# Another order for the first tiles of a hybrid decoder block: tokens 256 to 511 first, meta tokens later

## The chip, the cores and the metric

The kernel runs on one core of a Trainium2 chip. Its time is the device time of one execution in microseconds, and lower is better. The kernel before takes 1662.32 us (median of 3 runs, 1662.05 to 1663.47).

## What is computed

The reference is one layer of a decoder with three parallel mixers, and a SwiGLU after it. 16 meta tokens are put ahead of 1024 tokens, each of 1024 channels.

```
u = rms_norm(h, norm_mix)                       # h: 1040 x 1024
proj = u @ w_in                                 # q, k, v of two attentions, forget logits, xc, yc, gates
o_a = sliding-window attention (sinks, relative bias); o_f = forgetting attention
o_c = rg_lru(conv(xc)) * gelu(yc)               # xc, yc: 512 channels each
merged = sum over g of sigmoid(gates[g]) * (o_g @ w_branch[g])
h = h + merged @ w_out
h = h + (silu(gate) * up) @ w_ffn_out           # of rms_norm(h, norm_ffn) @ w_ffn_in
out = rms_norm(h, norm_final), meta tokens dropped
```

The change is in the first stage alone: the norm of the 1040 tokens, and the first parts of the projections to xc and yc.

## The kernel before

The tokens are cut into nine tiles: tile 0 has the 16 meta tokens, tiles 1 to 8 have 128 tokens each. For each tile `load_x` brings the rows from HBM into one of four buffers `xt` (512 KB by one DMA; tile 0 has 64 KB). `normed` takes the sum of squares on ScalarE (L297), a square root (L298) and, on VectorE, a reciprocal (L299) and two halves of x times the factor times the gain (L301, it reads `xt` and `gbc`, the gain copied to all partitions by a DMA of 512 KB). `to_feature_major` turns the tile on TensorE: four transposes of 128x128 into a PSUM bank, twice (L204); there are two such banks. Each bank is copied to `uh` on ScalarE (L118), and what is lost to the shorter type `fp32r` goes to `ul` on VectorE (L119), by a subtraction that reads PSUM and `uh`.

A product is made of three matmuls for each of eight blocks of 128 channels (`mm3`, L150): high by high, high by low, low by high. Weights are split too: `load_w` loads 128x1024 numbers (512 KB) into one of two buffers `wr`, makes the high part on ScalarE (L137) and, for the first four weight tiles, the low part on GpSimd (L138), which reads two tensors in SBUF.

`proj_chunk` makes one chunk of a projection, 24 matmuls into one of three PSUM banks, and a `sink` copies the bank out on ScalarE (L269 for x, L272 for y). FULL has the chunks of all 1040 tokens: columns 0 to 271 (tiles 0, 1, 2), 272 to 527 (tiles 3, 4) and the last 512 (tiles 5 to 8). REAL leaves the meta tokens out: 512 columns, then the last 512.

All DMAs go through one queue, issued in order by SyncE (L58). The program order of the stage before is: load tiles 0, 1, the gain, tile 2; norm and turn them; four small loads and one matmul for the bias table (L321); two weights wx; load tiles 3, 4 and norm them; x of FULL[0] with the turns of tiles 3 and 4 between; x of FULL[1]; tiles 5 and 6 and two weights wy; y of REAL[0] for the first 128 channels; tiles 7 and 8; y of REAL[0] for the second; x of FULL[2]; y of REAL[1]. Each engine runs its own list in order, but the lists are made by a scheduler that follows estimated times beside the program order: matmuls of both x weights alternate in the trace. After the stage come the recurrence beside more projections, the attentions, the merge and the feed-forward part, which are not edited.

Of the kernel before, what the change touches and what calls it, by code (L numbers as in the profile page):

```python
# [16 lines left out]
P = 128  # L17
D = 1024
KT = D // P
NM = 16  # L20
# [14 lines left out]
QA, KA, QF, KF, XC, YC, GT = 0, 4, 5, 9, 13, 17, 21  # L35
# [16 lines left out]
def hybrid_block(ctx, tc, h_in, w_in, w_v0, w_v1, w_bd, par, rows, gains, relt, onehot,  # L52
                 maskrow, cmask, w_br, w_out, w_fi, w_fo, out):
    nc = tc.nc
    act, dve, pool, pe = nc.scalar, nc.vector, nc.gpsimd, nc.tensor
# [33 lines left out]
    o_bank = lambda label="": bank("ob", 1, label)  # L89
# [6 lines left out]
    ident = cp.tile([P, P], F32, name="ident")  # L96
# [29 lines left out]
    def load_w(src, n, pl=None, tag="w", bufs=None, lo_on_pool=False):  # L126
        pl = pl or wp
        kw = {} if bufs is None else dict(bufs=bufs)
        if n == D:
            raw = wp.tile([P, n], F32, tag="wr", name=nm("wr"))  # L130
        else:
            raw = pl.tile([P, n], F32, tag=tag + "r", name=nm(tag + "r"), **kw)
        dma(raw, src)
        hi = pl.tile([P, n], F32R, tag=tag + "h", name=nm(tag + "h"), **kw)
        lo = pl.tile([P, n], F32R, tag=tag + "l", name=nm(tag + "l"), **kw)
        if lo_on_pool:
            act.activation(hi, raw, AF.Copy)  # L137
            pool.tensor_tensor(lo, raw, f32(hi), ALU.subtract)  # L138
        else:
            split(hi, lo, raw)  # L140
        return hi, lo
# [12 lines left out]
    def run(gen):  # L154
        for _ in gen:
            pass
# [41 lines left out]
    def to_feature_major(xg, n, uh, ul, off):  # L198

        for half in range(2):  # L200
            pt = tr_bank()
            for i in range(4):
                k = 4 * half + i
                pe.transpose(pt[:, i * P:i * P + n], xg[:n, k * P:(k + 1) * P], ident[:n, :n])  # L204
            src = pt.rearrange("p (i q) -> p i q", i=4)[:, :, :n]
            ks = slice(4 * half, 4 * half + 4)
            split(uh[:, ks, off:off + n], ul[:, ks, off:off + n], src)
# [9 lines left out]
    FULL = ((0, 0, 272, 0), (0, 272, 256, 272), (1, 0, 512, 528))  # L217
    REAL = ((0, NM, 512, 0), (1, 0, 512, 512))

    def proj_chunk(j, w, chunk, sink):  # L220
        c, off, n, t0 = chunk
        ps = mm_bank(f"_w{j}")
        yield from mm3(ps[:, :n], [(w[0][:, k * P:(k + 1) * P], w[1][:, k * P:(k + 1) * P],
                                    uh[c][:, k, off:off + n], ul[c][:, k, off:off + n]) for k in range(KT)])
        sink(ps, n, t0)
# [36 lines left out]
    def x_sinks(pl, m):  # L262
        xr = pl.tile([P, 3 + T], F32, tag="xr", bufs=4, name=nm("xr"))
        y = pl.tile([P, S], F32, tag="y", bufs=4, name=nm("y"))
        pool.memset(xr[:, 0:3], 0.0)
        lru_in[m] = (xr, y)

        def xsink(ps, n, t0):
            act.activation(xr[:, 3 + t0:3 + t0 + n], ps[:, :n], AF.Copy)  # L269

        def ysink(ps, n, t0):
            act.activation(y[:, t0:t0 + n], ps[:, :n], AF.Copy)  # L272
        return xsink, ysink
# [3 lines left out]
    with tc.tile_pool(name="r0", bufs=1, side="right", reuse_waits="tile") as r0:  # L277
        gbc = r0.tile([P, D], F32, name="gbc")

        def rows_of(t):  # L280
            return (NM, 0) if t == 0 else (P, NM + (t - 1) * P)

        def load_x(t):
            n, t0 = rows_of(t)
            xt = r0.tile([P, D], F32, tag="xt", bufs=4, name=nm("xt"))
            dma(xt[:n], h_in[t0:t0 + n])
            return xt

        def norm_in(t, xt):
            to_feature_major(*normed(t, xt))  # L290

        def normed(t, xt):
            n, t0 = rows_of(t)
            c, off = (0, t0) if t0 < W0 else (1, t0 - W0)
            xg = r0.tile([P, D], F32, tag="xg", bufs=3, name=nm("xg"))
            q = cp.tile([P, 1], F32, tag="sq", bufs=4, name=nm("sq"))
            act.activation(xg[:n], xt[:n], AF.Square, accum_out=q[:n])  # L297
            act.activation(q[:n], q[:n], AF.Sqrt, bias=epst[:n], scale=1.0 / D)  # L298
            dve.reciprocal(q[:n], q[:n])  # L299
            for x, y, z in zip(*(halves(v[:n]) for v in (xg, xt, gbc))):  # L300
                dve.scalar_tensor_tensor(x, y, q[:n], z, ALU.mult, ALU.mult)  # L301
            return xg, n, uh[c], ul[c], off

        xts = [load_x(t) for t in range(2)]
        dma(gbc, gains[0:1].partition_broadcast(P))
        xts.append(load_x(2))
        n0, n1 = normed(0, xts[0]), normed(1, xts[1])
        to_feature_major(*n1)
        n2 = normed(2, xts[2])
        to_feature_major(*n0)  # L310
        to_feature_major(*n2)

        dma(cmt, cmask)
        rt = r0.tile([32, 8], F32, name="rt")
        oh = r0.tile([32, 383], F32, name="oh")
        mr = r0.tile([8, 383], F32, name="mr")
        dma(rt, relt)
        dma(oh, onehot)
        dma(mr, maskrow.partition_broadcast(8))
        pb = sc_bank()  # L320
        pe.matmul(pb[:8, :383], rt, oh, start=True, stop=True)  # L321
        dve.tensor_tensor(mr, pb[:8, :383], mr, ALU.add)
        sinks = [x_sinks(ra, m) for m in range(2)]
        wx = [load_w(w_in[XC + m], D, r0, f"x{m}", lo_on_pool=True) for m in range(2)]
        xs34 = [load_x(t) for t in (3, 4)]
        n34 = [normed(t, xs34[t - 3]) for t in (3, 4)]
        for m in range(2):
            run(proj_chunk(XC + m, wx[m], FULL[0], sinks[m][0]))
            if m == 0:
                to_feature_major(*n34[0])  # L330
                to_feature_major(*n34[1])
        for m in range(2):
            run(proj_chunk(XC + m, wx[m], FULL[1], sinks[m][0]))
        xs56 = [load_x(t) for t in (5, 6)]
        wy = [load_w(w_in[YC + m], D, lo_on_pool=True) for m in range(2)]
        for t in range(5, 7):
            norm_in(t, xs56[t - 5])
        run(proj_chunk(YC, wy[0], REAL[0], sinks[0][1]))
        for t in range(7, 9):
            norm_in(t, load_x(t))  # L340
        dma(part, par)
        dma(rowt, rows.partition_broadcast(P))
        dve.tensor_scalar(nsink, rowt[:, 0:8], -1.0, None, ALU.mult)
        dma(bts, mr)
        pad(r0, 32)
        bb = r0.tile([P, 8, 383], F32, name="bb")
        dma(bb, bts.partition_broadcast(P))
        dma(bss, bb)
        run(proj_chunk(YC + 1, wy[1], REAL[0], sinks[1][1]))
        for m in range(2):  # L350
            run(proj_chunk(XC + m, wx[m], FULL[2], sinks[m][0]))
        for m in range(2):
            run(proj_chunk(YC + m, wy[m], REAL[1], sinks[m][1]))
# [868 lines left out]
```

## Time and profile before

| | |
|---|---|
| median of the runs | 1662.32 us |
| the profiled execution | 1662.29 us |
| its span (first to last instruction) | 1660.5 us |
| TensorE busy with matmuls | 1630.2 us, 98% |
| VectorE, ScalarE, GpSimd busy | 60%, 46%, 26% |
| TensorE's first instruction | 9.07 us |
| TensorE's first projection matmul | 15.39 us |
| mean granted clock of TensorE | 0.996 |

The span is shorter than the execution by 1.8 us, which lie ahead of the first and behind the last instruction. In the rows below a time is the start in microseconds from the span's start, then follow the duration, engine, line and operation, with the tile written, an arrow and the tiles read. Brackets give how long the engine was idle before and what ended that.

### The profile page before, as it was taken

The numbers are of one execution on the slowest core, as the hardware profiler recorded it, in microseconds if no ns is written. First come the engines' busy times: TensorE is split into PE (matmuls) and PEld (weight loads), VectorE is DVE, ScalarE is ACT, GpSimd is POOL, SyncE is SP. The second block draws the span as 40 slices with busy tenths as digits, with TensorE's granted clock in tenths as the row PEclk, the third lists the DMA queues.
The fourth block names the chain that finished last, engine by engine and source line by source line (L and its number), as shares of the span: only waits on it lengthen the run. The fifth ranks groups of instructions, "written<-read, shape, count | busy, mean of one in ns | idle before, by whom it ended". The sixth has DMA issues, their size and how long they took to land.

```text
span 1660.5 us, 22597 instructions
## 1 busy us (share of the span) xinstructions
PE 1630.2 (98%) x8159; PEld 1375.1 (83%) x8159; DVE 999.4 (60%) x1799; ACT 760.7 (46%) x1397; POOL 433.1 (26%) x341
## 2 busy tenths in 40 slices
PE   7999999999999999999999999899999999999998
PEld 6898978888888888888887888688888888888886
DVE  6565556555566666641348437977666676567544
ACT  6456466555555555542336434333333333345342
POOL 2111001001122221110225001776666566300000
PEclk9999999999999999999999999899999999999999
DMA  7132352223324142339737221464444443598642
GB/s 255 63 108 93 122 153 79 88 89 121 108 76 129 59 122 79 107 114 320 244 127 235 102 77 70 158 222 169 165 147 146 146 161 131 197 356 278 195 128 101
DMA packets 110879, 242.47 MB, mean 146 GB/s; under 512 B 11944, under 2 KB 23544, under 8 KB 110512
## 3 DMA queue, kind: packets, MB, share of 16 engines
q1 hardware_dynamic: 110768, 241.04, 42.7%
q8 instruction: 64, 1.05, 0.3%
q14 instruction: 47, 0.39, 0.1%
HBM read 163.45 MB, written 72.21 MB: 142 GB/s over the span
## 4 chain that ended last, share of the span: by engine, by line
PE 87%; DVE 4%; issue 4%; ACT 2%; POOL 1%; DMA 1%; SPq 0%; DVEq 0%; POOLq 0%; ACTq 0%
PE mm_w L150 26%; PE mm_s L150 13%; PE tr_s L150 7%; PE mm_br L150 6%; PE mm_wo L150 5%; PE mm_x L1086 4%; PE tr_y L1086 4%; PE sc_y L1086 4%; PE ob L547 3%; PE sc_s L150 3%; PE tr L558 3%; PE mm_v L150 2%; PE ob_x L1086 1%; PE mm_g L150 1%; PE mm_u L150 1%
## 5 line engine op out<-in xcount | busy, mean ns | idle before, releaser
L150 PE MATMUL mm_w<-uh,wh 128*128 128x512 f32 (+2 forms) x744 | 292.6, 393 | 0.0
L150 PE MATMUL mm_w<-uh,wl 128*128 128x512 f32 (+2 forms) x744 | 280.5, 377 | 0.0
L150 PE MATMUL mm_w<-ul,wh 128*128 128x512 f32 (+2 forms) x744 | 279.9, 376 | 0.0
L150 PEld LDWEIGHTS mm_w<-uh,wl 128*128 128x128 f32 x744 | 140.0, 188 | 25.7
L150 PEld LDWEIGHTS mm_w<-uh,wh 128*128 128x128 f32 x744 | 140.4, 189 | 12.7
L150 PEld LDWEIGHTS mm_w<-ul,wh 128*128 128x128 f32 x744 | 140.7, 189 | 11.7
L119 DVE TENSOR_TENSOR ab<-raw,ab 128x1024 fp32r<-128x1024 f32 x77 | 93.0, 1224 | 71.6 <-ACT ab L118 69.6
L118 ACT ACTIVATE ab<-raw 128x1024 fp32r<-128x1024 f32 x77 | 80.9, 1059 | 94.7 <-PE ob_x L1086 23.4
L150 PE MATMUL mm_s<-pt,ar 128*128 128x512 f32 x480 | 117.4, 394 | 3.7 <-ACT c L952 3.7
L118 ACT ACTIVATE wh<-wr 128x1024 fp32r<-128x1024 f32 (+1 forms) x85 | 72.7, 856 | 103.2 <-PE mm_w L150 50.6
L150 PE MATMUL mm_br<-o,wh 128*128 128x512 f32 x384 | 118.3, 389 | 0.0
L119 DVE TENSOR_TENSOR pl<-tr,ph 128x384 fp32r<-128x384 f32 (+2 forms) x160 | 87.4, 555 | 47.0 <-ACT ph L118 43.1
L150 PEld LDWEIGHTS mm_s<-pt,ar 128*128 128x128 f32 x480 | 91.5, 191 | 23.6 <-ACT c L952 4.5
L118 ACT ACTIVATE ph<-tr 128x384 fp32r<-128x384 f32 (+2 forms) x160 | 76.8, 485 | 53.6 <-PE tr L558 51.5
L119 DVE TENSOR_TENSOR wl<-wr,wh 128x1024 fp32r<-128x1024 f32 x45 | 55.6, 1235 | 72.2 <-ACT wh L118 71.9
L648 POOL TENSOR_SCALAR s<-s,sm 128x144 f32<-128x144 f32 (+3 forms) x64 | 48.6, 761 | 172.1 <-DVE sm L647 144.2
L150 PEld LDWEIGHTS mm_br<-o,wh 128*128 128x128 f32 x384 | 72.1, 188 | 14.9
L558 PE MATMUL tr<-ident,s 128*128 128x128 f32 x480 | 79.6, 274 | 1.2 <-POOL s L596 0.6
L150 PE MATMUL mm_wo<-woh,hl 128*128 128x512 f32 x256 | 79.1, 390 | 0.0
L150 PE MATMUL mm_br<-o,wl 128*128 128x512 f32 x192 | 75.3, 392 | 1.5 <-DVE wl L119 1.4
L558 PEld LDWEIGHTS tr<-ident,s 128*128 128x128 f32 x480 | 59.1, 140 | 18.3 <-DVE pl L119 3.4
L1086 PE MATMUL mm_x<-ab 128*128 128x512 f32 x297 | 72.7, 389 | 0.0
(252 smaller groups left out, 3687.9 us busy)
## 6 DMA issues: line engine op xcount, KB each, us to landing
wr<-w_in_dram SPq DMA_DIRECT2D x45, 512.0 KB, 3.7
wr<-w_fi_dram SPq DMA_DIRECT2D x44, 512.0 KB, 3.8
raw<-asp SPq DMA_DIRECT2D x77, 256.0 KB, 3.2
asp<-a SPq DMA_DIRECT2D x66, 256.0 KB, 2.5
gz<-z SPq DMA_DIRECT2D x48, 256.0 KB, 2.1
o<-osp SPq DMA_DIRECT2D x24, 512.0 KB, 6.1
sg<-gz SPq DMA_DIRECT2D x48, 256.0 KB, 3.2
fo<-w_fo_dram SPq DMA_DIRECT2D x22, 512.0 KB, 5.1
```

Source lines behind the costliest of these rows:

```text
L118: act.activation(hi, src, AF.Copy)
L119: i = dve.tensor_tensor(lo, src, f32(hi), ALU.subtract)
L150: pe.matmul(ps, a, b, start=first and i == 0, stop=i == n - 1, skip_group_check=not first)
L547: pe.matmul(ob[:, q0:q0 + b - a], vt[:, c], x[:, a:b], start=count == 0, stop=count == n_mm - 1, skip_group_check=True)
L558: pe.transpose(tb[:, col:col + P], src, ident)
L648: pool.tensor_scalar(s[:, :nk], s[:, :nk], den, 1.0, ALU.mult, ALU.mult)
L1086: pe.matmul(banks[x], a[:, 0, q], b[:, 1], start=first and j == 0 and c == 0, stop=j == NJ - 1 and c % 3 == 2, skip_group_check=True)
```

## The change

Tiles 3 and 4 are loaded, normed and turned first, and x of FULL[1] is projected before the other tiles are used. The two weights wx are loaded behind tile 4, ahead of tiles 0, 1 and 2; then come tiles 1, 2 and 0, with the two weights wy loaded ahead of them. y of tokens 256 to 511 comes next, then the small loads and the matmul of the bias table, x of FULL[0], tiles 5 to 8, and y of tokens 0 to 255: the 512-column chunk REAL[0] of y has become two of 256. Besides, TensorE gets 32 transposes into a PSUM bank that nobody reads: 16 of the identity matrix at the beginning, and 8 of the normed tile after each of tiles 3 and 4.

```diff
-        xts = [load_x(t) for t in range(2)]
+        def busy(x, n, k):
+            for i in range(k):
+                pe.transpose(spare[:, :n], x[:n, i * P:(i + 1) * P], ident[:n, :n])
+
+        spare = o_bank("_spare")
+        for _ in range(16):
+            busy(ident, P, 1)
+
+        xts = {3: load_x(3)}
         dma(gbc, gains[0:1].partition_broadcast(P))
-        xts.append(load_x(2))
-        n0, n1 = normed(0, xts[0]), normed(1, xts[1])
-        to_feature_major(*n1)
-        n2 = normed(2, xts[2])
-        to_feature_major(*n0)
-        to_feature_major(*n2)
+        xts[4] = load_x(4)
+        wx = [load_w(w_in[XC + m], D, r0, f"x{m}", lo_on_pool=True) for m in range(2)]
+        sinks = [x_sinks(ra, m) for m in range(2)]
+        for t in (3, 4):
+            n = normed(t, xts[t])
+            to_feature_major(*n)
+            busy(n[0], P, 8)
+        xts = {t: load_x(t) for t in range(3)}
+        wy = [load_w(w_in[YC + m], D, lo_on_pool=True) for m in range(2)]
+        for m in range(2):
+            run(proj_chunk(XC + m, wx[m], FULL[1], sinks[m][0]))
+        for t in range(1, 3):
+            norm_in(t, xts[t])
+        norm_in(0, xts[0])
+        for m in range(2):
+            run(proj_chunk(YC + m, wy[m], (0, 272, 256, 256), sinks[m][1]))
...
-        sinks = [x_sinks(ra, m) for m in range(2)]
-        wx = [load_w(w_in[XC + m], D, r0, f"x{m}", lo_on_pool=True) for m in range(2)]
-        xs34 = [load_x(t) for t in (3, 4)]
-        n34 = [normed(t, xs34[t - 3]) for t in (3, 4)]
         for m in range(2):
             run(proj_chunk(XC + m, wx[m], FULL[0], sinks[m][0]))
-            if m == 0:
-                to_feature_major(*n34[0])
-                to_feature_major(*n34[1])
+        for t in range(5, 9):
+            norm_in(t, load_x(t))
         for m in range(2):
-            run(proj_chunk(XC + m, wx[m], FULL[1], sinks[m][0]))
-        xs56 = [load_x(t) for t in (5, 6)]
-        wy = [load_w(w_in[YC + m], D, lo_on_pool=True) for m in range(2)]
-        for t in range(5, 7):
-            norm_in(t, xs56[t - 5])
-        run(proj_chunk(YC, wy[0], REAL[0], sinks[0][1]))
-        for t in range(7, 9):
-            norm_in(t, load_x(t))
+            run(proj_chunk(YC + m, wy[m], (0, NM, 256, 0), sinks[m][1]))
...
-        run(proj_chunk(YC + 1, wy[1], REAL[0], sinks[1][1]))
```

## Rows read from the trace of the kernel before

**Rows 1.** The page's first part, TensorE's share of the span, and the first line of the chain of work that ended last.

```profile
PE 1630.2 (98%) x8159; PEld 1375.1 (83%) x8159; DVE 999.4 (60%) x1799; ACT 760.7 (46%) x1397; POOL 433.1 (26%) x341
PE 87%; DVE 4%; issue 4%; ACT 2%; POOL 1%; DMA 1%; SPq 0%; DVEq 0%; POOLq 0%; ACTq 0%
```

**Rows 2.** The table of waits of TensorE over the whole span: who waited for whom, us in total, times, longest.

```profile
PE tr L204 <- DVE xg L301: 9.1, 1, 9.1
...
PE tr L204 <- DVE ul L119: 0.5, 1, 0.5
```

**Rows 3.** The timeline of TensorE from 9 to 16 us: all up to the first projection matmuls.

```profile
9.07 1.94 PE L204 MATMUL tr<-ident,xg 128*128 128x128 f32 x8 [9.07 <-DVE xg L301]
10.94 1.44 PE L321 MATMUL sc<-oh,rt 32*8 32x383 f32 x2
12.31 3.25 PE L204 MATMUL tr<-ident,xg 16*128 16x16 f32 x16
15.39 0.59 PE L150 MATMUL mm_w<-uh,x0h 128*128 128x272 f32 x1
15.78 0.43 PE L150 MATMUL mm_w<-uh,x1h 128*128 128x272 f32 x1
```

**Rows 4.** The timeline of VectorE from 0 to 21 us, the instructions of the first norms and turns.

```profile
6.86 2.73 DVE L301 SCALAR_TENSOR_TENSOR xg<-xt,sq,gbc 16x512 f32<-16x512 f32 x4 [0.45 <-DMA gbc<-gains_dram]
10.14 0.16 DVE L299 RECIPROCAL sq<-sq 128x1 f32<-128x1 f32 x1 [0.55 <-ACT sq L298]
10.34 0.75 DVE L301 SCALAR_TENSOR_TENSOR xg<-xt,sq,gbc 128x512 f32<-128x512 f32 x1
11.01 0.68 DVE L119 TENSOR_TENSOR ul<-tr,uh 128x512 fp32r<-128x512 f32 x1
11.61 0.74 DVE L301 SCALAR_TENSOR_TENSOR xg<-xt,sq,gbc 128x512 f32<-128x512 f32 x1
12.27 0.68 DVE L119 TENSOR_TENSOR ul<-tr,uh 128x512 fp32r<-128x512 f32 x1
...
16.22 0.69 DVE L119 TENSOR_TENSOR ul<-tr,uh 128x512 fp32r<-128x512 f32 x1 [0.16 <-ACT uh L118]
```

**Rows 5.** The timeline of ScalarE, of the same stretch: the square of tile 2, the copies out of the transposes' banks, and the high parts of the weights (those of wy are from 24 us on).

```profile
8.63 1.06 ACT L297 ACTIVATE xg<-xt 128x1024 f32<-128x1024 f32 x1 [2.42 <-DMA xt<-h_in_dram]
...
10.19 0.60 ACT L118 ACTIVATE uh<-tr 128x512 fp32r<-128x512 f32 x1
11.04 0.60 ACT L118 ACTIVATE uh<-tr 128x512 fp32r<-128x512 f32 x1 [0.26 <-PE tr L204]
11.54 1.05 ACT L137 ACTIVATE x0h<-wr 128x1024 fp32r<-128x1024 f32 x1
...
14.74 0.60 ACT L118 ACTIVATE uh<-tr 128x512 fp32r<-128x512 f32 x1
...
24.57 1.05 ACT L137 ACTIVATE wh<-wr 128x1024 fp32r<-128x1024 f32 x1
```

**Rows 6.** The timeline of SyncE's queue from 0 to 60 us: when DMAs were issued.

```profile
4.47 0.83 SPq L58 DMA_DIRECT2D wr<-w_in_dram  x2
6.73 6.00 SPq L58 DMA_DIRECT2D xt<-h_in_dram  x4
15.05 2.67 SPq L58 DMA_DIRECT2D wr<-w_in_dram  x2
```

**Rows 7.** From the view of the tile wr, in stretches that hold one issue each: the time from issue to landing of the first weight load (issued at 4.47) and of the third (issued at 15.05).

```profile
DMA to landing us min/median/max: 5.7/5.7/5.7
...
DMA to landing us min/median/max: 4.2/4.2/4.2
```

**Rows 8.** The table by stretches of 1 us: busy time of PE, PEld, DVE, ACT and POOL, granted clock, DMA share and GB/s.

```profile
8.00:9.00 1.00, 0.00 (x0) 0.00 (x0) 1.00 (x3) 0.37 (x1) 0.00 (x0) 1.00 1.03 347
9.00:10.00 1.00, 0.93 (x5) 0.96 (x6) 0.59 (x1) 0.97 (x3) 0.00 (x0) 1.00 1.02 418
```

**Rows 9.** Timelines of TensorE in short stretches: a transpose alone and three in a row early on, eight in a row later.

```profile
10.59 0.42 PE L204 MATMUL tr<-ident,xg 128*128 128x128 f32 x1
...
14.28 0.85 PE L204 MATMUL tr<-ident,xg 128*128 128x128 f32 x3
...
20.64 1.03 PE L204 MATMUL tr<-ident,xg 128*128 128x128 f32 x8
```

**Rows 10.** Timelines of TensorE in short stretches: pairs of projection matmuls, of 272 columns early and later, of 256 and of 512 columns.

```profile
16.73 0.43 PE L150 MATMUL mm_w<-uh,x0h 128*128 128x272 f32 x1
16.96 0.43 PE L150 MATMUL mm_w<-ul,x0h 128*128 128x272 f32 x1
...
19.45 0.35 PE L150 MATMUL mm_w<-uh,x0h 128*128 128x272 f32 x1
...
19.89 0.28 PE L150 MATMUL mm_w<-uh,x0h 128*128 128x272 f32 x1
20.01 0.29 PE L150 MATMUL mm_w<-ul,x0h 128*128 128x272 f32 x1
...
25.49 0.28 PE L150 MATMUL mm_w<-ul,x0h 128*128 128x256 f32 x1
25.61 0.28 PE L150 MATMUL mm_w<-uh,x0l 128*128 128x256 f32 x1
...
32.34 0.39 PE L150 MATMUL mm_w<-uh,wl 128*128 128x512 f32 x1
32.57 0.39 PE L150 MATMUL mm_w<-uh,wh 128*128 128x512 f32 x1
```

**Rows 11.** Timelines of GpSimd (the low parts of the weights) and of VectorE in the stretch of the last two.

```profile
12.67 2.35 POOL L138 TENSOR_TENSOR x0l<-wr,x0h 128x1024 fp32r<-128x1024 f32 x1 [11.28 <-ACT x0h L137]
14.99 2.37 POOL L138 TENSOR_TENSOR x1l<-wr,x1h 128x1024 fp32r<-128x1024 f32 x1
25.70 2.42 POOL L138 TENSOR_TENSOR wl<-wr,wh 128x1024 fp32r<-128x1024 f32 x1 [8.33 <-ACT wh L137]
28.07 2.86 POOL L138 TENSOR_TENSOR wl<-wr,wh 128x1024 fp32r<-128x1024 f32 x1
...
28.59 2.88 DVE L301 SCALAR_TENSOR_TENSOR xg<-xt,sq,gbc 128x512 f32<-128x512 f32 x1
```

## The prediction

> **What bounds the kernel now.** I read the page's busy shares and chain first, then TensorE's waits, then the first 35 us engine by engine. TensorE is busy 98% of the span and holds 87% of the chain [rows 1]: nearly every microsecond in which it has no useful work, or does it slowly, is on the path, and one that is won early reaches the end unless a later wait takes it back. Its longest wait of all is the first, 9.1 us for the first normed half tile; the other wait of this stage is 0.5 us [rows 2]. The front costs more than the 9.1 us. Up to the first projection matmul at 15.39 TensorE runs only 24 transposes (tiles 1, 0 and 2) and the bias-table matmul [rows 3]. [...]
>
> What sets 15.39 is a chain with tile 2 at its end, not the weights. The gain lands at 6.86, and VectorE makes the four halves of tiles 0 and 1 (2.73 us) [rows 4]. Tile 2 lands just before 8.63 [rows 5]; its halves are made at 10.34 and 11.61, each with a low part of tile 1 behind it, up to 12.95 [rows 4]. These low parts free the two transpose banks. Tile 0 passes through the banks next, and the copy of tile 2's first half ends at 15.34 (14.74 + 0.60) [rows 5], 0.05 us ahead of the matmul. The low weight part x0l was done at 15.02 (12.67 + 2.35) [rows 11], only 0.4 us earlier.
>
> **The change part by part.** All terms are against the profiled execution, 1662.29 us (span 1660.5 and 1.8 around it); it lies 0.03 us below the median of 1662.32, so no correction is made.
>
> (a) The first matmul. The new chain has two tiles and no tile 0 between them. In front of tile 4 the queue now moves tile 3 and the gain, 1024 KB; before, 64 + 512 + 512 = 1088 KB stood ahead of tile 2, at 350 to 420 GB/s [rows 8] a difference of 0.2 us, so tile 4 lands at about 8.4. Square, root and reciprocal take what they took (8.63 to 10.30), so its halves are made at about 10.1 and 11.4, alternating with tile 3's low parts as at 10.34 to 12.95 [rows 4]. Tile 3's first low part frees a bank at 11.5; four cold transposes 0.21 us apart ((0.85 - 0.42) / 2; the first and the last of three, [rows 9]) and their latency, a copy of 0.60: the first half is ready for matmuls at about 13.4. The first weight now has 1536 KB ahead of it instead of 1725, which at the same rate is 0.5 us; it landed at 10.2 (4.47 + 5.7, [rows 6, 7]), so now at 9.7; ScalarE took it only at 11.54, behind copies [rows 5]. With the same delay x0l ends at about 14.5, without it 13.2. The third matmul or so needs x0l. On TensorE the eight dummy transposes of tile 4 stand ahead of the matmuls in the program: cold 8 x 0.21 = 1.7 us. Those that fit between the turns of tile 4's halves are free, the others are not: if all run behind its second half, the first matmul is at about 15.1. Between 13.4 and 15.1 I take the middle, 14.2: -1.2 us. The other dummies cost nothing: 16 x 0.21 = 3.4 us lie before the first norm (TensorE is idle to 9.07), and tile 3's eight lie before tile 4's turns.
>
> (b) Slow matmuls. From 15.39 to 19.45 there are 16 matmuls (the first 3 with waits, 13 at 0.23) [rows 3, 10], worth 16 x 0.122 = 1.95: 2.1 us lost. [...]
>
> (c) Work that lay ahead of the first matmul and now lies behind it. Tiles 1 and 2 change places with 3 and 4: nothing. Tile 0's eight small turns and the two bias-table matmuls now run in dense time: at least 8 x 0.05 + 2 x 0.3 = 1.0, half of what they took cold (the two matmuls started 0.6 apart), at most 8 x 0.11 + 2 x 0.3 = 1.5: +1.2.
>
> (d) y in two chunks. Before, 48 matmuls of 512 columns, 0.23 apart; after, 96 of 256, 0.12 apart [rows 10]: 96 x 0.12 - 48 x 0.23 = 11.5 - 11.0, from the unrounded starts +0.6. The two more copies are ScalarE's and are hidden by the next chunk.
>
> (e) The wait of 0.5 us [rows 2] stood between tiles 5 and 6, where low weight parts held VectorE up; tiles 5 to 8 now come after GpSimd has done them: -0.5, at worst 0.
>
> (f) SyncE. wy0 and wy1 wait for the buffers that x0l and x1l free (before: issued at 15.05 and 17.4, [rows 6]); the bias-table loads and tiles 5 to 8 queue behind them. The table is read in the attentions, far behind; tiles 5 to 8 are due only after 96 matmuls of y and x and 24 transposes, 14 us of TensorE. Tile 2 waits for tile 3's buffer, free at about 8. Nothing on the path: 0, at worst the second rival.
>
> (g) VectorE beside GpSimd. A multiply of L301 takes 0.75 us, but 2.88 while GpSimd makes a low weight part, ending 0.55 after it; a low part of L119, which reads PSUM, stays at 0.69 in such a stretch [rows 4, 11]. Tiles 1 and 2 are now normed while x1l and wy's low parts are made, up to 2.1 us late each. The 48 x matmuls (6 to 10 us) cover it: 0, at worst +2.
>
> Sum: -1.2 - 0.3 + 1.2 + 0.6 - 0.5 = -0.2, so 1662.1 us: the start that is won is paid back by what was moved behind it. With (a) from -2.0 to +1.1 (an x0l that ends at 14.5 or a half of tile 4 held up by it as in (g)), (c) from 1.0 to 1.5 and (e), (g) at their bounds, this case reaches from 1660.5 to 1664.5.
>
> **The rivals.** First: the dummies raise the clock. [...] For it: TensorE would have work from about 1.6 us on. Against it: before, transposes and two small matmuls filled most of 9.07 to 15.39 without any rise, and the rise came after 4 us of projection matmuls [rows 3, 10]. [...] The trace agrees as far as it goes, but its early transposes are broken by gaps and small tiles, so I leave the rival a quarter.
>
> Second, on the slower side: TensorE waits for y's weights. y of tokens 256 to 511 stands ahead of x of FULL[0] in the program. TensorE is through with 48 x matmuls and 24 turns at about 14.2 + 4.1 + 29 x 0.12 + 2.4 = 24.2. wy0 is issued when x0l is done (13.2 to 14.5), lands 4.2 later [rows 7], needs 1.05 on ScalarE and 2.4 on GpSimd [rows 5, 11]: 20.9 to 22.2 if ScalarE takes it at once. But ScalarE also has three squares, five copies and the weights then, and before it took wy0 only at 24.57, with the low part done at 28.1 [rows 5, 11]. The point is 24.2; at 28.1 the wait is 3.9 us: 1666.0. Against it: the scheduler can put x of FULL[0] first.
>
> Third, the change doesn't do what it says: the scheduler puts the tiles or dummies in another order, for instance all dummies at cold speed into time with work, 1664; or a later stage is planned otherwise, up to 3 us either way.
>
> **How the numbers follow.** Forecast 0.54, the clock 0.24, y's weights 0.13, another order 0.09. What a measurement of this kernel can tell from no change is 0.2%, 3.3 us: below 1659.0 or above 1665.6. Faster: a third of the clock case (with a start at 13.4, or less moved behind it), 0.08, half of the other order, 0.04, and 0.06 of the forecast's own edge: 0.18. Slower: half of the wait case and a third of the other order, 0.10, and 0.04 of the forecast: 0.14. No change: 0.68. The range holds the clock case nearly whole and half of the wait case: 1658.6 to 1665.4.
>
> **What would show it.** (a): the first mm_w of 256 columns at 13.4 to 15.1. (b): its successors 0.21 apart for some 4 us, then 0.12; 0.12 from the first says that the dummies raised the clock. (c), (d): 96 y matmuls of 256 columns 0.12 apart, and tile 0's turns between dense work. (e): no TensorE wait on ul near tiles 5 and 6. (g): multiplies of over 2 us beside x1l or wl. The second rival would be an idle TensorE between 20 and 28 us, ended by GpSimd's wl. I am wrong if TensorE's first 45 us hold over 3.3 us more or less useful work than before, or if the difference arises after that.

## The result, and the profile after

The kernel after the change takes 1667.68 us, the median of 6 executions (1666.36 to 1669.16); the kernel before beside it on the same chip takes 1662.18 (6 executions, 1660.75 to 1663.47). The ratio is 1.0034, 95% interval 1.0021 to 1.0047. The forecast was 1662.1 and its range ended at 1665.4: the change costs 5.5 us where none were expected, and the prediction is wrong. The profiled executions have spans of 1665.3 and 1660.5 us, so 4.8 of the 5.5 us can be looked for in the two traces; the profiled execution of the kernel after (1667.10 us) lies 0.6 below the median of its six.

TensorE's line on the page, beside [rows 1]:

```profile
PE 1635.5 (98%) x8239; PEld 1382.5 (83%) x8239; DVE 1000.2 (60%) x1799; ACT 760.9 (46%) x1399; POOL 434.8 (26%) x341
```

It holds 80 pairs of weight load and matmul more (32 transposes that nobody reads, 48 matmuls from y in two chunks), and 5.3 us more of busy time. The table of TensorE's waits (us in total, times, longest), beside [rows 2]:

```profile
PE tr L204 <- DVE ul L119: 3.8, 2, 2.3
...
PE tr L204 <- DVE xg L301: 2.2, 1, 2.2
...
PE sc L590 <- DVE sm L592: 1.3, 1, 1.3
```

The first wait of 9.1 us has become one of 2.2, but two new waits on low parts (ul) have come, and one in an attention. Three places follow from that. The first is the wait of 2.3 us; the timeline of ScalarE from 7 to 16 us, beside [rows 5]:

```profile
8.84 0.30 ACT L298 ACTIVATE sq<-sq,epst 128x1 f32<-128x1 f32 x1
9.04 1.04 ACT L137 ACTIVATE x0h<-wr 128x1024 fp32r<-128x1024 f32 x1
10.64 1.06 ACT L137 ACTIVATE x1h<-wr 128x1024 fp32r<-128x1024 f32 x1 [0.56 <-DMA wr<-w_in_dram]
11.61 1.06 ACT L118 ACTIVATE uh<-tr 128x512 fp32r<-128x512 f32 x2
12.56 1.06 ACT L297 ACTIVATE xg<-xt 128x1024 f32<-128x1024 f32 x1
...
13.70 0.60 ACT L118 ACTIVATE uh<-tr 128x512 fp32r<-128x512 f32 x1
14.76 0.60 ACT L118 ACTIVATE uh<-tr 128x512 fp32r<-128x512 f32 x1 [0.47 <-PE tr L204]
```

In this stretch ScalarE works its list in order: tile 3's transposes were through at 9.3, but their copies (11.61) stand behind both high weight parts, and x1h waits 0.56 us for its DMA with the copies behind it. Tile 4's copies (13.70, 14.76) stand behind the square of tile 1 (12.56) too, but that cost next to nothing: the first four transposes of tile 4 ended only at 13.66. VectorE's timeline, beside [rows 4]:

```profile
9.37 1.42 DVE L301 SCALAR_TENSOR_TENSOR xg<-xt,sq,gbc 128x512 f32<-128x512 f32 x2
12.22 1.29 DVE L119 TENSOR_TENSOR ul<-tr,uh 128x512 fp32r<-128x512 f32 x2 [1.44 <-ACT uh L118]
14.33 0.69 DVE L119 TENSOR_TENSOR ul<-tr,uh 128x512 fp32r<-128x512 f32 x1 [0.82 <-ACT uh L118]
...
17.94 5.40 DVE L301 SCALAR_TENSOR_TENSOR xg<-xt,sq,gbc 128x512 f32<-128x512 f32 x2
...
24.83 1.27 DVE L119 TENSOR_TENSOR ul<-tr,uh 128x512 fp32r<-128x512 f32 x2
```

Tile 4's halves are ready at 10.8 (9.37 + 1.42), earlier than tile 2's were, but the two transpose banks come free only with the low parts that start at 12.22. And at 17.94 the two multiplies of tile 2 take 5.40 us in place of 1.42. GpSimd makes the low parts of y's weights just then:

```profile
17.60 5.19 POOL L138 TENSOR_TENSOR wl<-wr,wh 128x1024 fp32r<-128x1024 f32 x2 [2.29 <-ACT wh L137]
```

What TensorE saw of both, beside [rows 3] (the timeline of TensorE; x8 and the like are instructions in one stretch):

```profile
9.06 1.63 PE L307 MATMUL ob_spare<-ident,xg 128*128 128x128 f32 x9
12.96 0.70 PE L204 MATMUL tr<-ident,xg 128*128 128x128 f32 x4 [2.27 <-DVE ul L119]
...
15.66 0.56 PE L150 MATMUL mm_w<-uh,x0h 128*128 128x256 f32 x1
...
25.56 0.66 PE L204 MATMUL tr<-ident,xg 128*128 128x128 f32 x4 [1.55 <-DVE ul L119]
```

The first projection matmul comes at 15.66, not at 14.2; and a second stop of 1.55 us comes at 24 us, ahead of tile 2's turns. The third place lies 220 us later. SyncE's queue and VectorE in the kernel before:

```profile
235.11 0.33 SPq L58 DMA_DIRECT2D wr<-w_in_dram  x1
...
237.15 2.17 SPq L58 DMA_DIRECT2D v<-vs  x2
...
243.19 0.37 DVE L586 CUSTOM_DVE_ANT_0 s<-sc,nb,nsink 128x144 f32<-128x144 f32 x1 [1.73 <-DMA nb<-bss]
```

and in the kernel after, 2.7 us later by the clock of the trace:

```profile
237.80 0.98 SPq L58 DMA_DIRECT2D wr<-w_in_dram  x1
...
239.84 3.06 SPq L58 DMA_DIRECT2D v<-vs  x2
...
247.84 0.37 DVE L592 CUSTOM_DVE_ANT_0 s<-sc,nb,nsink 128x144 f32<-128x144 f32 x1 [3.69 <-DMA nb<-bss]
```

One issue of a weight load holds SyncE 0.98 us instead of 0.33 and the next two 3.06 instead of 2.17; so the first bias block nb, which the attention's first scores need, is issued 0.9 us later against the rest (242.95 instead of 239.37, where the weight load came 2.7 later), and VectorE can use it 4.9 us after its issue instead of 3.8. VectorE waits 2 us longer for it, and TensorE 1.3 us for VectorE (the third row of the waits above). The instructions and their order are the same in both kernels from about 50 us on, on every engine.

Two measures sum this up. The first splits TensorE's time up to the first matmul of x's last chunk (512 columns, program line 351 of before), from the start times of all its records. The second is the lag: the start of an instruction of TensorE less the start of the same one (counted from the last) in the kernel before.

```
TensorE to x's last chunk, us    start+dummies+idle  transposes  bias table     x      y    sum
before                                  9.70            9.46        1.37     14.12  11.73  46.38
after                                  14.12            8.52        0.74     12.36  13.06  48.81

lag of after, us, at    60 us: 2.78    230: 2.69    260: 4.22    560: 5.40    760: 5.22    end: 4.81
```

So 2.7 us come from the front, 1.5 from the place near 244 us, and 0.6 from small steps behind it. 2.43 of the front's 2.7 us are there when x's last chunk starts (48.81 less 46.38). Split at the first projection matmul they are: that matmul +0.27; x -1.75; y +1.33; the stop of 1.55 new and one of 0.53 gone; the rest, the turns of tile 0 and the bias table that moved behind it, +1.56.

### The profile page after: what moved, and what is told of

It is laid out like the page before. It is cut to its first block, busy times and chain, and to the rows that moved or that the text cites. A ratio compares the mean times of both kernels' runs of the same rounds, so it can differ in the third digit from the quotient of the medians.

```text
span 1665.3 us, 22764 instructions
## 1 busy us (share of the span) xinstructions
PE 1635.5 (98%) x8239; PEld 1382.5 (83%) x8239; DVE 1000.2 (60%) x1799; ACT 760.9 (46%) x1399; POOL 434.8 (26%) x341
## 3 DMA queue, kind: packets, MB, share of 16 engines
q8 instruction: 65, 1.06, 0.3%
## 5 line engine op out<-in xcount | busy, mean ns | idle before, releaser
L150 PEld LDWEIGHTS mm_s<-pt,ar 128*128 128x128 f32 x480 | 91.0, 190 | 22.6 <-ACT c L958 3.6
```

Of the source, the lines that this page charges most:

```text
L150: pe.matmul(ps, a, b, start=first and i == 0, stop=i == n - 1, skip_group_check=not first)
```

## The experiments

Ten kernels ran. The table gathers them; pairs are TensorE's instruction pairs more than before, the step is the lag at 260 us less that at 230, all from one profiled execution each, and the ratio, from all executions, is to the kernel before on the same chip. Executions of one kernel lie 2 to 5 us apart from the fastest to the slowest, so the lags of a single one are not its median: start_dummies_old_order ends 0.24 us behind in the profiled execution, the fastest of its 11, and 2.0 behind in the median.

```
                             first mm  x's last  lag at  step at  lag at   pairs   ratio, 95% interval
                                         chunk    60 us    244      end
before                         15.39     46.38     0        0        0        0
after                          15.66     48.81    2.78     1.53     4.81     80    1.0034 [1.0021, 1.0047]
dummies_in_old_order           16.24     45.03   -1.35     0.03    -0.92     32    0.9996 [0.9987, 1.0004]
no_dummies                     13.19     47.27    1.24     0.64     4.01     48    1.0016 [1.0008, 1.0025]
copies_first                   13.60     49.46    3.42     1.81     5.92     80    1.0041 [1.0027, 1.0055]
low_on_vectore                 16.09     48.23    2.19     1.44     3.15     80    1.0015 [1.0006, 1.0024]
both_waits                     13.72     46.38    0.35     1.33     0.66     80    1.0009 [1.0001, 1.0018]
y_in_two_old_order             16.43     45.83   -0.52     1.02     0.41     80    1.0006 [0.9997, 1.0015]
more_dummies                   15.81     49.93    3.90     0.49     5.31     96    1.0026 [1.0015, 1.0036]
more_dummies_low_on_vectore    15.88     48.36    2.33     0.04     3.39     96    1.0023 [1.0014, 1.0033]
both_waits_more_dummies        14.03     49.15    3.12     0.01     2.20     96    1.0014 [1.0006, 1.0023]
start_dummies_old_order        17.31     47.30    0.92     0.51     0.24     36    1.0015 [1.0006, 1.0024]
```

**The dummies alone, and the order alone.** The first pair splits the change in two. dummies_in_old_order adds to the kernel before only

```
+        spare = o_bank("_spare")
+        for _ in range(16):
+            busy(ident, P, 1)
         ...
         to_feature_major(*n1)
+        busy(n1[0], P, 8)
         ...
         to_feature_major(*n2)
+        busy(n2[0], P, 8)
```

> The kernel before with the 32 transposes that nobody reads added (16 of the identity at the beginning, 8 after the turn of tile 1, 8 after that of tile 2) and nothing moved. Theory A (the new order costs the time, by two waits: tile 3's copies queue behind the second weight's high part on ScalarE, and tile 2's multiplies are held up by GpSimd's low parts): the dummies are harmless or help a little, by raising the clock before 19.5 us: 1660 to 1663, ratio to before 0.999 to 1.0005. Rival B (the dummies cost it, by standing ahead of real work on TensorE and by longer code): 1664 to 1668. Rival C (the 2.4 us that the changed kernel loses between 220 and 700 us, where its instruction order is the old one, come from moved code positions): then this kernel too, whose TensorE list is 64 instructions longer, shows a shift that grows by 1 to 3 us there; by A it grows by under 1.

It took 1661.01 us, ratio 0.9996: no difference that can be told, by the profile 0.9 us ahead. no_dummies is the kernel after without them:

```
-        spare = o_bank("_spare")
-        for _ in range(16):
-            busy(ident, P, 1)
         ...
-            busy(n[0], P, 8)
```

> The changed kernel without the 32 transposes that nobody reads. Without them the scheduler puts tile 3's copies ahead of the second weight's high part on ScalarE. Theory A: the first projection matmul comes at 13 to 14 us instead of 15.7, but at the lower clock for about 4 us, and tile 2's turn still waits for a low part of GpSimd, so TensorE's start of x of FULL[2] comes at 47.5 to 49.5 (48.8 changed, 46.4 before): 1665 to 1668. Rival B (the dummies cost it): back to 1661 to 1663.

It took 1664.91 us, 2.5 behind before's 1662.37 in that comparison. x's last chunk came at 47.27, just ahead of what I expected. So the new order loses without the dummies too, though not all of it: 2.5 us by the medians where the kernel after lost 5.5 (4.0 and 4.8 by the profiles). In the old order the dummies cost nothing that can be told; in the new one the kernel with them is the slower. The run also showed two things of the prediction. Without the dummies the scheduler puts tile 3's copies ahead of x1h, and the first matmul comes at 13.19: dummies that TensorE has time for change the plan of the other engines. And TensorE then waits 1.29 us for GpSimd's low part of y's weights, the prediction's second rival, at a third of its price:

```profile
23.20 0.38 PE L150 MATMUL mm_w<-uh,wl 128*128 128x256 f32 x1 [1.29 <-POOL wl L138]
```

**ScalarE's list.** copies_first moves two things in ScalarE's list, x1h behind tile 3's copies and the squares of tiles 1 and 2 behind tile 4's:

```
+                with tc.issue_after(last):
+                    act.activation(x1h, raw1, AF.Copy)
         ...
-            norm_in(t, xts[t])
+            with tc.issue_after(last):
+                n = normed(t, xts[t])
+            to_feature_major(*n)
```

> The changed kernel with ScalarE's order pinned: the second weight's high part x1h behind tile 3's copies, the squares of tiles 1 and 2 behind tile 4's copies. Theory A: the first projection matmul comes at 13.0 to 14.0 instead of 15.66 and the clock, once up at 10 us, stays up; but tile 2's turn still waits for GpSimd's last low part, so most is lost again there: start of x of FULL[2] at 47.5 to 49 (48.8 changed), time 1665.5 to 1668. If ScalarE's order were the whole cause, x of FULL[2] would start at 46 or earlier and the time would be 1662 to 1664.5.

The first matmul came 2.1 us earlier (13.60), yet the kernel stayed as slow, 1668.21 us. Its VectorE and GpSimd timelines say where it went:

```profile
17.79 5.36 DVE L303 SCALAR_TENSOR_TENSOR xg<-xt,sq,gbc 128x512 f32<-128x512 f32 x2
```

```profile
17.45 5.15 POOL L140 TENSOR_TENSOR wl<-wr,wh 128x1024 fp32r<-128x1024 f32 x2 [2.21 <-ACT wh L139]
```

Now tile 1 is the one held up, and TensorE, earlier by 2 us, waits 1.06 us for its first half and 2.13 us for its second:

```profile
20.55 0.63 PE L206 MATMUL tr<-ident,xg 128*128 128x128 f32 x4 [1.06 <-DVE xg L303]
...
23.30 1.09 PE L206 MATMUL tr<-ident,xg 128*128 128x128 f32 x4 [2.13 <-DVE sq L301]
```

ScalarE's list is not the whole cause. The clock did not come as expected either: up at 12.72 us, not 10, and down again from 22.96 to 26.38, beside the second of these stops.

**VectorE held by GpSimd.** low_on_vectore makes y's low parts on VectorE:

```
-        wy = [load_w(w_in[YC + m], D, lo_on_pool=True) for m in range(2)]
+        wy = [load_w(w_in[YC + m], D) for m in range(2)]
```

> The changed kernel with the low parts of the two weights wy made on VectorE instead of GpSimd. Theory A: no multiply of tile 2 of over 2 us any more, TensorE's wait of 1.55 us before tile 2's turn goes, start of x of FULL[2] at 46.8 to 47.6 (48.8 changed): 1665 to 1666.5, 1 to 2 us below the changed kernel. If the wait has another cause (ScalarE's copies, late loads), it stays and the time with it: 1667 to 1668.

The stop of 1.55 us went, and the kernel took 1664.57 us: some 3 us better than after by the ratios, still 2.2 behind before. The first stop (2.27 us at 10.70) stayed. But x's last chunk came at 48.23, not at 46.8 to 47.6. Much of what the stop gave back went to the clock: in this execution it rose at 5.38 us, fell at 8.79 and was back only at 19.03, 2.9 us after the first matmul (16.09), so that x took 13.15 us instead of 12.36. Two rows of the table by stretches (busy shares and counts of PE, PEld, DVE, ACT, POOL; granted clock, DMA share, GB/s):

```profile
9.00:10.00 1.00, 1.00 (x5) 0.63 (x3) 0.81 (x2) 1.00 (x2) 0.00 (x0) 0.50 1.10 352
...
18.00:19.00 1.00, 1.00 (x6) 1.00 (x6) 1.00 (x2) 1.00 (x3) 0.00 (x0) 0.50 1.04 150
```

The 11 executions of this kernel have mean granted clocks from 0.994 (this one) to 0.998, so the time at the lower clock differs between executions of one kernel. both_waits puts the last two edits together.

> Two edits of the kernel after together: the two of copies_first, and y's first weights split on VectorE as in low_on_vectore. Theory (two waits in series, ScalarE's list before the first projection matmul and VectorE held by GpSimd before tile 2's turn, and each hides what the other's removal brings): first projection matmul at 13.6 as in copies_first, the waits of 1.06 and 2.13 us at 19.5 and 21.2 us gone, so the first matmul of x's last chunk at 49.46 - 3.2 = 46.3 us or earlier (a drop of the clock at 23 us would go too, up to 1.5 us more), level with before's 46.38. Rival (the wait only moves on to another producer): that matmul stays later than 48 us. The step of 1.5 us near 244 us stays in either case, since the 80 more instruction pairs stay: end 1.4 to 2 us behind before.

x's last chunk starts at 46.38, before's own figure. One stop of 1.21 us is left, at 21.2 us, for tile 2's multiplies, which now stand behind a weight's low part in VectorE's own list. At x's last chunk the edit of ScalarE's list alone lost 0.65 us against after (49.46 against 48.81), the one of VectorE alone won 0.58, and both together won 2.43. The multiplies in both_waits, run beside no GpSimd:

```profile
21.52 1.41 DVE L303 SCALAR_TENSOR_TENSOR xg<-xt,sq,gbc 128x512 f32<-128x512 f32 x2
```

The two waits stand in series on the same path. Without the first alone, the second grew (from 1.55 to 3.19 us in two stops); without the second alone, TensorE still stopped at 10.7 us, and the low clock took half of the gain (0.79 of 1.55 us). Together the clock rose at 12.80, ahead of the first matmul, and stayed up. The lag at the end, 0.66, is less than I expected (1.4 to 2), since 0.5 us are won back between 540 and 600 us and as much between 1040 and 1080; the median was 1663.67, 0.95 us behind before's 1662.72.

**The step at 244 us.** With the front even, both_waits has it still, dummies_in_old_order has not. A packet of 16 KB on a queue of instructions (q8 on the page; the times of single packets are read from the trace) falls within about 1 us ahead of the slow weight-load issue: in after it starts at 236.80 and takes 1.37 us. In before the nearest are at 229.20 and 253.04. The page counts 64 such packets before and 65 after:

```profile
q8 instruction: 64, 1.05, 0.3%
```

```profile
q8 instruction: 65, 1.06, 0.3%
```

That is one per 255 instructions of TensorE (2 x 8159 / 64), and 253 in after (2 x 8239 / 65), so the packets are taken for fetches of TensorE's code; that is an inference from these counts, no run shows it alone. If it holds, more pairs at the front make a later fetch fall earlier in the work: the eleventh packet of the span starts 17.9 us behind the issue in before (253.04 and 235.11) and 1.0 ahead of it in after (236.80 and 237.80). y_in_two_old_order tests it: the old order, the old loads, the same 80 pairs.

```
-        run(proj_chunk(YC, wy[0], REAL[0], sinks[0][1]))
+        run(proj_chunk(YC, wy[0], (0, 272, 256, 256), sinks[0][1]))
+        run(proj_chunk(YC, wy[0], (0, NM, 256, 0), sinks[0][1]))
```

(the same for wy[1], and the 32 dummies of dummies_in_old_order).

> The kernel before with 32 transposes that nobody reads (as in dummies_in_old_order) and y's first 512 columns in two chunks: 80 more pairs of instructions on TensorE than before, as many as after has, with the old order of tiles and loads. Theory (the step near 244 us comes from where the fetches of TensorE's code fall): the lag on before is about -1.35 + 1.3 = 0 at 60 us, rises by 1.5 us between 230 and 260 us, and ends near +1.5. Rival (the step comes from the new order of the loads): no step, lag from 0 at 60 us to between 0 and +0.5 at the end. Apart from that the run measures y in two chunks: 0.6 us by the prediction, 1.3 by the account of after.

The step came, 1.02 us against 0.03 with 32 pairs, with the same marks on SyncE and VectorE. It is smaller than the 1.5 that I expected, and so is the lag at the end, 0.41; the kernel took 1662.88 us beside before's 1662.72:

```profile
234.53 1.20 SPq L58 DMA_DIRECT2D wr<-w_in_dram  x1
```

```profile
244.07 0.37 DVE L599 CUSTOM_DVE_ANT_0 s<-sc,nb,nsink 128x144 f32<-128x144 f32 x1 [3.19 <-DMA nb<-bss]
```

It also prices y in two chunks: y's matmuls take 12.20 us instead of 11.75, and x's last chunk comes 0.8 us later. more_dummies goes the other way, 16 pairs more than after, with 24 dummies behind tile 3:

```
-            busy(n[0], P, 8)
+            for _ in range(3 if t == 3 else 1):
+                busy(n[0], P, 8)
```

> The kernel after with 24 instead of 8 transposes that nobody reads behind tile 3. Theory (the wait of 2.28 us at 10.7 us is ScalarE's and VectorE's and stays, but TensorE filled over it keeps the full clock): first projection matmul 15.5 to 16.2, no fall of the clock at 13.45, first matmul of x's last chunk 1 to 2 us earlier than after's 48.81. With 96 more pairs than before the code fetch comes some 4 us earlier by the theory of the code's place: the step between 230 and 260 us falls from 1.5 to under 0.7. Rival (the step comes with any lag of TensorE): it stays 1.5. Rival on the clock (transposes don't hold it): it falls near 13 us as in after and the last chunk is as late, or later by the 16 transposes' time.

> As more_dummies, and y's first weights split on VectorE as in low_on_vectore. Theory: both the wait before tile 2's turn (1.55 us) and the slow clock go: first matmul of x's last chunk at 46 to 47 us, the level of before (46.38), and no step near 244 us, so an end within 1 us of before's. Rival (what is won in one place is waited for in the next): that matmul stays at 48 us or later, the end 2 us or more behind before's.

The second has low_on_vectore's edit too. The steps are 0.49 and 0.04 us with lags of 3.84 and 2.29 at 230 us, so a late TensorE alone does not make the step. The issue in the second is quick again, and the wait short:

```profile
237.39 0.33 SPq L58 DMA_DIRECT2D wr<-w_in_dram  x1
```

```profile
245.68 0.37 DVE L593 CUSTOM_DVE_ANT_0 s<-sc,nb,nsink 128x144 f32<-128x144 f32 x1 [1.93 <-DMA nb<-bss]
```

Over all kernels: with 80 pairs that issue takes 0.58 to 1.20 us and the step is 1.0 to 1.8, in either order; with any other count it takes 0.33 and the step is 0 to 0.64; that load lands 4.9 to 6.5 us after its issue with 80 pairs and 3.8 to 4.1 with others. With 96 pairs the packet falls near as well, but it has ended 0.7 us or more ahead of the issue; with 80 it is still running then, or has just ended (both_waits, 0.13 us ahead, with the shortest of the slow issues, 0.58). What makes the small ones (0.49 to 0.64) is open: there the issue is quick, but nb lands late all the same. The fronts of these two kernels missed: x's last chunk came 1.1 us later than in after in the one, 0.45 earlier in the other, whose rival came true (48.36, and 3.4 us behind before at the end). The scheduler answered the longer list with other places for ScalarE's work: in more_dummies the square of tile 2 too went ahead of tile 4's copies, and TensorE waited 0.52 us for its first matmul and 1.01 us two matmuls later, with the clock down again from 18.28 to 21.69.

**Two tries at a kernel better than both.** both_waits_more_dummies is both_waits with 26 dummies at the start and 14 behind tile 4; start_dummies_old_order is the kernel before with 36 at the start and no others.

```
-        for _ in range(16):
+        for _ in range(26):
             busy(ident, P, 1)
         ...
             busy(n[0], P, 8)
+            if t == 4:
+                busy(n[0], P, 6)
```

> As both_waits, with 26 instead of 16 transposes that nobody reads ahead of tile 3 (over the 2.3 us in which TensorE waited at 5.1 us) and 14 instead of 8 behind tile 4 (over the wait for the first projection matmul): 96 more instruction pairs than before, as in more_dummies_low_on_vectore. Theory of the code's place: the step between 230 and 260 us, 1.33 us in both_waits, falls under 0.3. First matmul of x's last chunk at 45.5 to 46.4 us (the clock rises earlier, the producers set the rest), so an end 0.3 to 1.2 us ahead of before's. Rival (the step belongs to the new order with a front as fast as before's): it stays near 1.3, the end 0.5 to 1 us behind before's. Rival on the front: six more transposes ahead of the first projection matmul push it by 0.6 us and all behind it.

```
+        for _ in range(36):
+            busy(ident, P, 1)
```

> The kernel before with 36 transposes of the identity that nobody reads at the very start and none behind the tiles: the old order alone, with TensorE busy from 1.4 to 9 us. Theory (the transposes pay by the clock alone, and the old order is as good as the new): the clock rises ahead of 12.8 us, the first projection matmul comes ahead of dummies_in_old_order's 16.24, by 15.4 as before's or earlier, and the first matmul of x's last chunk 0.3 to 1 us ahead of dummies_in_old_order's 45.03; 36 more pairs, no step near 244 us; end 1 to 2 us ahead of before's. Rival (VectorE and ScalarE set the old front and not TensorE): the last chunk stays at 45 us or later, the end within 1 us of before's.

Neither is faster than before. In the first the step is gone (0.01 us), as foretold, which a rival tied to the new order does not allow; but VectorE's list had a weight's low part (1.23 us) ahead of tile 2's multiplies, TensorE stopped for 1.91 us at 22.6, and 3 us of lag came from there and the fall of the clock behind it. The second missed too: its first matmul came at 17.31. It shows the clock by transposes alone: the seven from 1.71 us on stand 0.21 us apart ((1.70 - 0.42) / 6), the eleven from 6.29 on 0.11.

```profile
1.71 1.70 PE L307 MATMUL ob_spare<-ident 128*128 128x128 f32 x7
...
6.29 1.36 PE L307 MATMUL ob_spare<-ident 128*128 128x128 f32 x11
```

Then TensorE waited 2.44 us, up to 13.45, for tile 1's low parts with nothing to run, and the granted clock went to 0.50 at 12.53. The table by stretches (busy shares and counts of PE, PEld, DVE, ACT, POOL; granted clock, DMA share, GB/s):

```profile
12.00:13.00 1.00, 0.00 (x0) 0.00 (x0) 0.39 (x1) 1.00 (x4) 1.00 (x1) 0.77 1.05 418
13.00:14.00 1.00, 0.55 (x4) 0.50 (x4) 0.90 (x2) 1.00 (x3) 1.00 (x2) 0.50 1.02 406
18.00:19.00 1.00, 1.00 (x6) 1.00 (x6) 0.68 (x2) 1.00 (x3) 0.00 (x0) 0.50 0.96 225
20.00:21.00 1.00, 1.00 (x11) 1.00 (x10) 0.96 (x3) 0.79 (x1) 0.14 (x1) 1.00 0.54 209
```

The clock bought early was lost again before a projection matmul used it. In dummies_in_old_order TensorE ran turns and dummies without a gap from 9.17 us on, the clock rose at 12.77 and stayed up; there x takes 12.16 us instead of 14.12, the largest part of what that kernel gains.

## Why the prediction was wrong, point by point

**(a) The first matmul: -1.2 expected, +0.27 measured.** Two steps failed. Tile 4's halves were indeed ready earlier (10.8), but the step "tile 3's first low part frees a bank at 11.5" took the order of ScalarE's list from before, where the copies stood ahead of x0h [rows 5]. With the weights' loads early in program order, ScalarE took both weights first, and a low part came only at 12.9 (12.22 and half of 1.29). So the first half of tile 4, which I had ready for matmuls at 13.4, was copied at 14.30 (13.70 + 0.60). The second is the dummies behind tile 4. I had taken half of their price, 0.8 us with the turns; six of the eight ran cold (0.50 granted) behind the second half's turns, from 14.52 to 15.66, while what the first matmuls read was ready (x0l since 12.98). That makes 1.36 us from 14.30 on, 0.56 more than I took. With x1h behind tile 3's copies the term lay within its bounds of 13.4 to 15.1: 13.60 in copies_first and 13.72 in both_waits, 1.8 and 1.7 us ahead of before.

**(b) Slow matmuls: -0.3 expected, -1.75 measured, and the first rival.** The clock rose 1.2 us after the first matmul (0.57 granted from 16 to 17 us, 1.00 after), not 4.06 as in before (from 15.39 to 19.45, by the starts of the matmuls [rows 3, 10]). No run shows the term of -0.3, an estimate that takes before's 4.06 us over to after: 19 of x's 48 matmuls by the spacing of [rows 10] (0.23 x 256 / 272), and 29 behind them. In after the matmuls of 256 columns start 0.21 us apart from 16.02 to 16.87 and 0.12 from there on. Without the dummies (no_dummies) the clock rose at 16.68, 3.5 us after the first matmul. The rival's mechanism is real: in after dummies start 0.21 us apart up to 10.0 us and 0.11 from then on, with no projection matmul yet on the engine, and the granted clock falls only at 13.45, behind the stop of 2.27 us, as the table by stretches shows:

```profile
13.00:14.00 1.00, 1.00 (x7) 0.93 (x8) 0.51 (x1) 1.00 (x3) 1.00 (x1) 0.73 0.04 12
14.00:15.00 1.00, 1.00 (x7) 1.00 (x6) 0.67 (x1) 0.53 (x2) 1.00 (x1) 0.50 0.71 242
...
16.00:17.00 1.00, 1.00 (x8) 1.00 (x7) 0.96 (x4) 1.00 (x3) 0.00 (x0) 0.57 0.66 188
17.00:18.00 1.00, 1.00 (x11) 1.00 (x10) 0.83 (x3) 1.00 (x3) 0.40 (x1) 1.00 0.94 356
```

The 36 transposes of start_dummies_old_order show the rise by themselves, 0.21 us apart at first and 0.11 later. The gain that the rival hoped for did not come: the clock was down again when the first matmul came (0.50 granted from 15 to 16 us), so the dummies ahead of it stayed dear (0.21 us each), and what (b) won was less than what the other terms lost. How much (b) wins is partly luck: with the same dummies, low_on_vectore had the low clock for 2.9 us of matmuls.

**(c) Work moved behind the first matmul: +1.2 expected, +1.56 measured** (its bounds were 1.0 to 1.5). The mechanism holds, a little dearer.

**(d) y in two chunks: +0.6 expected, +1.33 in after, +0.45 alone** (+0.8 with what it pushes). As an edit by itself the term was about right; in after y's matmuls are also broken up more often by turns of tiles, and the account puts the slower start of the matmuls behind them on y.

**(e) -0.5 expected, -0.53 measured.** Right.

**(f) SyncE: 0 expected.** At the front right; wy0 was issued at 13.01, earlier than before, and in the kernel after TensorE did not wait for y's weights, as the second rival had it (it did in no_dummies).

**(g) VectorE held by GpSimd: 0 expected, +1.55 measured.** I had the row and the size (2.88 us a multiply [rows 11], here 2.7), and bounded it at +2, but took "the 48 x matmuls cover it" as its answer. The cover was 6.2 us (15.66 to 21.90) and the work under it longer: in VectorE's list the multiplies of tiles 1 and 2, with the hold, and tile 0's stood ahead of tile 1's low parts, from 16.19 to 24.83. A larger gain in (a) does not help: the earlier TensorE is, the thinner this cover, as copies_first showed. The traces show the hold as times alone: tile 2's two multiplies take 5.40 us beside GpSimd's 5.19, and 1.42 in low_on_vectore, where GpSimd makes no low part of y's weights; by what means was not shown.

**Behind the front: 0 expected, +1.5 and some 0.6 measured.** The prediction allowed "a later stage is planned otherwise", within the 0.09 of its third rival. No later stage is planned otherwise; the same lists run, but TensorE's list is longer and the 16-KB packets, taken for its code fetches, fall elsewhere (236.80 in after, 253.04 in before). The prediction had no term for that: the step came with 80 more pairs, in either order, and not with 96; that the fetch itself does it is inferred. What makes the rise of about 1 us between 500 and 520 us stays open. Of the later changes, 0.4 to 0.5 us are won back between 540 and 600 us by every one of the eleven kernels, so it is the trace of before that loses them there; and between 1040 and 1080 us, where the granted clock is at 0.50 for 6.8 to 10.2 us in every kernel, the lags jump by -0.6 to +0.8 us. The lag at the end is that uncertain.

Against the forecast of -0.2 the front went wrong by +2.6 us: +1.5 in (a), +1.55 in (g), +0.7 in (d), +0.4 in (c), less 1.45 that (b) won beyond its -0.3. A further 0.3 came up to 60 us, the step added 1.5, and the rest 0.6.

## What to carry to other kernels

Where several engines feed the first matmul, write down each engine's list in order before pricing a reordering: a term taken from the old trace holds only with the old neighbours in the list, and "covered" needs the length of the cover and of everything under it. Stops on one path can hide each other, so that two edits which each gain little or lose may together gain the whole. And instructions added at the front can cost far behind it, in a stage with equal lists: here 80 more pairs went with a step of 1.0 to 1.8 us some 220 us later, 96 with 0.01 to 0.49, so a kernel with a few instructions more or less tells.

## What was not expected of the hardware

Transposes alone raised TensorE's clock (0.213 us apart, 0.110 from 5.70 us on in start_dummies_old_order); it fell behind the stop of 2.27 us in after and within the one of 2.44 us there. A 16-KB fetch, taken for one of TensorE's instructions, beside SyncE's issue of a weight load went with an issue of 0.58 to 1.20 us instead of 0.33 and with that load landing 4.9 to 6.5 us after its issue instead of 3.8 to 4.1; that the fetch is the cause is inferred from the count of pairs and the order in time, since no kernel moved the fetch alone.
